# A two-layer hybrid transformer with two gated layers behind it: gate and value products by seven block products, retention and latent values by pairs of heads

## The chip, the cores and the metric

One core of a Trainium2 chip runs the whole program as one kernel. The metric is device time in microseconds of one execution, as a median over runs. Everything is float32; a large product is made of three matmuls of float32r (below), a small one is a plain float32 matmul.

## The reference

512 tokens of width 1024 pass two layers of attention and feed-forward and then two further layers (even and odd), which the change leaves alone. Each attention mixes three heads: a delta-rule recurrence (RWKV-7), a retention of four heads and a latent attention of eight. What the change touches:

```
# retention, four heads of 64, chunks of 128 tokens
inner = einsum('bhnqd,bhnkd->bhnqk', qc, kc) * dmask
inner = einsum('bhnqk,bhnkd->bhnqd', inner, vc)
cross = einsum('bhnqd,nbhde->bhnqe', qc * q_dec, R_prev)    # R_prev: state of the chunks before
# latent attention, eight heads, values of 64, blocks of 128 queries, causal
pr = softmax(s); o = einsum('bhqk,bkhd->bqhd', pr, v)
# feed-forward, D_FF = 2816
gu = rms_norm(h, ffn_norm[l]) @ w_gate_up[l]
h = h + (silu(gu[..., :D_FF]) * gu[..., D_FF:]) @ w_down[l]
```

## The kernel before

Activations stand with channels on the 128 partitions and the 512 tokens as columns. A product `w.T @ x` in full precision is three matmuls (`mm3`): `w` and `x` are each split in a rounded part (`h`) and a rest (`l`), and hh, hl and lh are added in PSUM. Weights come in units of 128 x 1024 (`wunit`): SP issues a transfer of 512 KB into `wr` (two buffers), ScalarE writes the rounded part `wh`, VectorE the rest `wl = wr - wh` (three buffers each). `dense_fm` is one such unit against eight pairs `xh`, `xl`: 24 matmuls of 512 columns into one PSUM bank.

**Feed-forward (`ffn`).** `prenorm` splits the eight channel blocks of `h` and makes the norm's factor, which is spread over the partitions as `RB` (and half of it as `RH`). The 22 blocks of 128 hidden channels go in groups of 8, 8 and 6. For each, one unit gives the gate `pg`, one the value `pu`; VectorE multiplies both, as they leave PSUM, by `RB` and `RH`, ScalarE makes the tanh of the silu, and the result is split (`fah`, `fal`). Behind each group come eight output products of 24 (or 18) matmuls each, added to `h`.

**Retention (`ret_states`, `ret_head`).** Two heads share a tile of 128 partitions. `ret_states` sums the states of the chunks into `R`, 64 columns a chunk. `ret_head` runs for one head: four score matmuls on its 64 partitions (`rsc`), a mask on VectorE, then per chunk one matmul with the state and one with the values into its half of the bank `ro`, and two evacuations by ScalarE.

**Latent attention (`mla_scores`, `mla_values`, `mla_queries`).** Per head and block of 128 queries: scores (`msc`), maximum on VectorE, exponential on ScalarE, normalization on VectorE. When a head has its four blocks, `mla_values` transposes the probabilities by key block (`mpt`) and multiplies them by the 128 value channels of the head's pair (`mo`); of the 128 output rows the head's own 64 are used:

```
self.mm(out[:, c0], st["v"][kb - 1][:, i * P:i * P + P], p0[:, c0], kb == 1, kb == NB)
```

**Order.** The program is written in order, and a scheduler puts instructions on each engine by priority; `high_priority` moves weight preparation (`WPRI`) and evacuations (`EPRI`) ahead. Each engine then runs its own list in order and waits on semaphores. In attention, `weave` puts the steps of the recurrence (`side`) between those of retention and latent attention (`main`). `VAT`, `QAT`, `VDELAY`, `QAHEAD`, `RPOST` say at which steps values, queries and the recurrence's end are issued.

Of the kernel before, what the change touches and what calls it, by code (L numbers as in the profile page):

```python
# [43 lines left out]
WEAVE, VAT, QAT, VDELAY, QAHEAD, RPOST = 1.9, (2, 6, 10, 14), 6, 1, 3, 20  # L44
MSCB, MOB, DB0, DB1, DB2 = ("pa", "pr", "pa", "pr"), "pd", ["pd", "pt"], ["pd"], ["pd"]
# [173 lines left out]
class _Kernel:  # L219
# [145 lines left out]
    def mm(self, out, lhsT, rhs, start, stop):  # L365
        self.nc.tensor.matmul(out=out, lhsT=lhsT, rhs=rhs, start=start, stop=stop)  # L366
# [451 lines left out]
    def rwkv_inverse(self, l, st, eng):  # L818
# [20 lines left out]
        for e in range(2):  # L839
            for hf in range(2):  # L840
                for b, q in enumerate((nc.sync, nc.scalar)):
                    o, i = 64 * hf + 32 * b + 16 * e, 64 * e + 32 * b + 16 * hf
                    q.dma_start(out=tt[i:i + 16, 16 * e:16 * e + 16, 32 * b:32 * b + 32], in_=s2[o:o + 16].rearrange("c i t -> i c t"))
# [155 lines left out]
    def ret_states(self, l, st):  # L999

        st["R"] = []
        for p in range(2):
            ps, kt = self.pt("rkt"), self.t("rkt", "X")
            for j in range(NB - 1):
                self.nc.tensor.transpose(ps[:, j * P:j * P + P], st["k"][p][:, j * P:j * P + P], self.ident)
            self.act(kt[:, :384], ps[:, :384])
            ps = self.pa("rkv")
            R = self.php.tile([P, 192], F32, tag=f"ret_r{p}", name="ret_r", bufs=1)
            for j in range(NB - 1):
                b = slice(j * P, j * P + P)  # L1010
                self.mm(ps[:, b], kt[:, b], st["v"][j][:, p * P:p * P + P], True, True)
                for e in range(2):
                    sl, c = slice(64 * e, 64 * e + 64), slice(64 * j, 64 * j + 64)
                    new = ps[sl, j * P + 64 * e:j * P + 64 * e + 64]
                    if j == 0:
                        self.nc.vector.tensor_copy(R[sl, c], new)
                    else:
                        self.add(R[sl, c], new, R[sl, 64 * j - 64:64 * j])
            st["R"].append(R)

    def ret_head(self, l, st, h):
        p, e = divmod(h, 2)
        sl = slice(64 * e, 64 * e + 64)
        if e == 0:
            st["y"], st["sq"] = st.get("y", []) + [self.t("ry", "M")], st.get("sq", []) + [self.t("rsq", "M")]
        ps, out, s = self.pa("rsc"), self.pt("ro"), self.t("rs", "X")
        k, q = st["k"][p], st["q"][p]
        blocks = [slice(j * P, j * P + P) for j in range(NB)]
        for b in blocks:
            self.mm(ps[:, b], k[sl, b], q[sl, b], True, True)  # L1030
        yield
        self.mul(s[:].rearrange("p (n t) -> p n t", t=P), ps[:].rearrange("p (n t) -> p n t", t=P),
                 self.co("upper").unsqueeze(1).to_broadcast([P, NB, P]))
        yield
        for j, b in enumerate(blocks):
            if j:
                self.mm(out[sl, b], st["R"][p][sl, 64 * j - 64:64 * j], q[sl, b], True, False)
            self.mm(out[sl, b], st["v"][j][:, h * 64:h * 64 + 64], s[:, b], j == 0, True)
        yield
        self.act(st["y"][p][sl], out[sl])  # L1040
        self.act(st["sq"][p][sl], out[sl], AF.Square)
        yield
# [97 lines left out]
    def mla_scores(self, qk, qb):  # L1140
# [3 lines left out]
        ps = self.bank(MSCB[qb], "msc")  # L1144
# [11 lines left out]
    def mla_values(self, l, st, h, prs, mix):  # L1156

        nc = self.nc
        i, e = divmod(h, 2)
        sl = slice(64 * e, 64 * e + 64)  # L1160
        if e == 0:
            mix.append((self.t("mxh", "M", F32R), self.t("mxl", "M", F32R)))
        pair = mix[-1]
        out, last = None, None
        for kb in range(NB + 1):
            if kb < NB:
                ps = self.pt("mpt")
                for qb in range(kb, NB):
                    nc.tensor.transpose(ps[:, qb * P:qb * P + P], prs[qb][:, kb * P:kb * P + P], self.ident)  # L1169
                pt = self.t("mpt", "R")  # L1170
                c = slice(kb * P, T)
                self.act(pt[:, c], ps[:, c])
            if last is not None:
                c0, p0 = last
                if out is None:
                    out = self.bank(MOB, "mo")
                self.mm(out[:, c0], st["v"][kb - 1][:, i * P:i * P + P], p0[:, c0], kb == 1, kb == NB)
            if kb < NB:
                last = (c, pt)
                yield  # L1180
        mh, ml = pair
        self.act(mh[sl], out[sl])
        self.sub(ml[sl], out[sl], mh[sl].bitcast(F32))

    def attn(self, l):
# [30 lines left out]
        def main():  # L1216
# [10 lines left out]
            heads = (x for h in range(4) for x in self.ret_head(l, rst, h))  # L1227
            qk = None
            for i, _ in enumerate(heads):
                if i in VAT:  # L1230
                    self.mla_v(l, mst, VAT.index(i))
                if i == QAT:
                    qk = self.mla_queries(l, mst, 0)
                if i % 4 == 3:
                    yield
# [5 lines left out]
            keys = {0: qk}  # L1241
            probs, vals, post = {}, [], iter(())
            for s in range(32 + VDELAY):
                h, qb = divmod(s, NB)
                if h < 8:
                    if qb == 0:
                        probs[h] = []
                    probs[h].append(self.mla_scores(keys[h], qb))
                if s >= NB + VDELAY and (s - VDELAY) % NB == 0:
                    i = (s - VDELAY) // NB - 1  # L1250
                    vals.append(self.mla_values(l, mst, i, probs[i], mix))
                vals = [v for v in vals if next(v, "end") != "end"]
                if (s + QAHEAD) % NB == 0 and NB <= s + QAHEAD < 32:
                    keys[(s + QAHEAD) // NB] = self.mla_queries(l, mst, (s + QAHEAD) // NB)
# [4 lines left out]
            vals.append(self.mla_values(l, mst, 7, probs[7], mix))  # L1259
# [15 lines left out]

    def ffn(self, l):
        self.dbanks = ["pd", "pt", "pr"]
        xs, rT, RB, RH = self.prenorm(f"ffn_norm{l}", half=True)
        for k0 in range(0, NF, 8):
            n = min(8, NF - k0)  # L1280
            acts = []
            for m in range(k0, k0 + n):
                pg = self.dense_fm(self.a["wgu"][l, 2 * m], xs)
                z = self.t("fz", "Z")
                self.evac(z, pg, RB)
                th = self.t("fth", "Z")
# [511 lines left out]
    def run(self):  # L1798
        self.setup()
        for l in range(L2):  # L1800
            with self.phase("attn", R=26, M=15, I=2):
                self.attn(l)
            with self.phase("ffn", F=40, Z=8):
                self.ffn(l)
# [47 lines left out]
```

## Time and profile before

| | us |
|---|---|
| median of 3 runs (2008.69 to 2012.46) | 2009.08 |
| profiled execution, its own time | 2010.3 |
| span of that execution, first to last instruction | 2008.5 |
| TensorE (PE) busy in the span | 1972.3 |
| VectorE (DVE) busy | 1274.5 |
| ScalarE (ACT) busy | 808.1 |
| GpSimd (POOL) busy | 68.9 |

A row of the timeline has its start, its duration and what it is: line, operation, `out<-in` by the program's names, shape. TensorE's durations overlap, since its matmuls are pipelined: what one costs is read from the starts. Row "x2" merges instructions of one kind. A line can be that of a helper: L285 is any tensor operation of two tensors, L303 one with a scalar besides, L306 any activation, L366 any matmul.

### The profile page before, as it was taken

The numbers are of one execution on the slowest core, as the hardware profiler recorded it, in microseconds if no ns is written. First come the engines' busy times: TensorE is split into PE (matmuls) and PEld (weight loads), VectorE is DVE, ScalarE is ACT, GpSimd is POOL, SyncE is SP. The second block draws the span as 40 slices with busy tenths as digits, with TensorE's granted clock in tenths as the row PEclk, the third lists the DMA queues.
The fourth block names the chain that finished last, engine by engine and source line by source line (L and its number), as shares of the span: only waits on it lengthen the run. The fifth ranks groups of instructions, "written<-read, shape, count | busy, mean of one in ns | idle before, by whom it ended". The sixth has DMA issues, their size and how long they took to land.

```text
span 2008.5 us, 25747 instructions
## 1 busy us (share of the span) xinstructions
PE 1972.3 (98%) x10016; PEld 1582.8 (79%) x10016; DVE 1274.5 (63%) x2367; ACT 808.1 (40%) x1323; POOL 68.9 (3%) x116
## 2 busy tenths in 40 slices
PE   8999999999999999999999999999999999999998
PEld 5777678888888877766788888888888888888886
DVE  7874665544535688647555354458988884389665
ACT  6523553322223444336433222234545453347242
POOL 3100000000000201000000000000000000020000
PEclk9999999999999999999999999999999999999999
DMA  5420122332332523212233233323333323222221
GB/s 178 127 69 23 52 85 91 99 94 95 96 103 87 166 85 102 52 33 70 74 95 95 95 97 103 95 86 98 97 94 98 100 90 112 93 72 84 74 84 43
DMA packets 64910, 180.06 MB, mean 90 GB/s; under 512 B 13892, under 2 KB 16740, under 8 KB 64788
## 3 DMA queue, kind: packets, MB, share of 16 engines
q1 hardware_dynamic: 60528, 175.27, 27.9%
q0 software_dynamic: 1808, 2.69, 0.5%
q8 instruction: 79, 1.29, 0.3%
q10 hardware_dynamic: 2452, 0.45, 0.2%
q14 instruction: 43, 0.35, 0.1%
HBM read 172.29 MB, written 6.09 MB: 89 GB/s over the span
## 4 chain that ended last, share of the span: by engine, by line
PE 81%; DVE 9%; issue 4%; ACT 3%; DMA 2%; POOL 1%; SPq 0%; DVEq 0%; ACTq 0%; POOLq 0%
PE pd L366 68%; PE msc L366 2%; PE mo L366 2%; DVE wl L285 2%; PE egate L366 1%; PE ro L366 1%; PE mpt L1169 1%; DVE xinv L285 1%; DVE xprod L285 1%; ACT wh L306 1%; PE bch L366 1%; DVE xl L303 1%; DMA wr<-owout 1%; PE ost L366 0%; DVE h L285 0%
## 5 line engine op out<-in xcount | busy, mean ns | idle before, releaser
L366 PE MATMUL pd<-xh,wh 128*128 128x512 f32 (+1 forms) x1512 | 591.2, 391 | 8.3 <-ACT xh L306 6.1
L306 ACT ACTIVATE wh<-wr 128x1024 fp32r<-128x1024 f32 (+3 forms) x285 | 296.3, 1040 | 746.7 <-PE pd L366 517.2
L366 PE MATMUL pd<-xl,wh 128*128 128x512 f32 (+1 forms) x1512 | 592.4, 392 | 4.3 <-DVE xl L303 4.1
L366 PE MATMUL pd<-xh,wl 128*128 128x512 f32 (+1 forms) x1512 | 590.2, 390 | 0.0
L285 DVE TENSOR_TENSOR wl<-wr,wh 128x1024 fp32r<-128x1024 f32 (+3 forms) x285 | 341.6, 1199 | 98.1 <-ACT wh L306 97.6
L366 PEld LDWEIGHTS pd<-xh,wh 128*128 128x128 f32 (+1 forms) x1512 | 284.2, 188 | 68.2 <-ACT xh L306 6.5
L366 PEld LDWEIGHTS pd<-xl,wh 128*128 128x128 f32 (+1 forms) x1512 | 284.3, 188 | 66.7 <-DVE xl L303 8.4
L366 PEld LDWEIGHTS pd<-xh,wl 128*128 128x128 f32 (+1 forms) x1512 | 284.4, 188 | 57.3 <-issue 1.0
L285 DVE TENSOR_TENSOR h<-pd,h 128x512 f32<-128x512 f32 x64 | 44.2, 691 | 150.1 <-PE pd L366 150.1
L366 PE MATMUL pd<-fal,wh 128*128 128x512 f32 x352 | 137.2, 390 | 0.0
L366 PE MATMUL pd<-fah,wl 128*128 128x512 f32 x352 | 137.0, 389 | 0.0
L366 PE MATMUL pd<-fah,wh 128*128 128x512 f32 x352 | 136.7, 389 | 0.0
L285 DVE TENSOR_TENSOR fth<-pd,RH 128x512 f32<-128x512 f32 x44 | 30.4, 692 | 118.6 <-PE pd L366 118.6
L366 PE MATMUL pd<-mxh,wh 128*128 128x512 f32 (+1 forms) x272 | 102.8, 378 | 0.0
L366 PE MATMUL pd<-mxh,wl 128*128 128x512 f32 (+1 forms) x272 | 102.6, 377 | 0.0
L366 PE MATMUL pd<-mxl,wh 128*128 128x512 f32 (+1 forms) x272 | 102.5, 377 | 0.0
L285 DVE TENSOR_TENSOR fz<-pd,RB 128x512 f32<-128x512 f32 x44 | 30.4, 692 | 99.3 <-PE pd L366 99.3
L366 PEld LDWEIGHTS pd<-fal,wh 128*128 128x128 f32 x352 | 66.1, 188 | 14.4 <-DVE fal L285 0.7
L366 PEld LDWEIGHTS pd<-fah,wh 128*128 128x128 f32 x352 | 66.0, 188 | 14.0 <-ACT fah L306 0.3
L366 PEld LDWEIGHTS pd<-fah,wl 128*128 128x128 f32 x352 | 66.1, 188 | 13.7
L366 PEld LDWEIGHTS pd<-mxh,wl 128*128 128x128 f32 x272 | 51.2, 188 | 9.3
L366 PEld LDWEIGHTS pd<-mxl,wh 128*128 128x128 f32 x272 | 51.2, 188 | 9.3
(509 smaller groups left out, 2851.4 us busy)
## 6 DMA issues: line engine op xcount, KB each, us to landing
wr<-wgu SPq DMA_DIRECT2D x88, 512.0 KB, 3.5
wr<-ewin SPq DMA_DIRECT2D x48, 512.0 KB, 3.5
wr<-win SPq DMA_DIRECT2D x35, 512.0 KB, 3.6
wr<-wd SPq DMA_DIRECT2D x32, 512.0 KB, 3.5
wr<-wout SPq DMA_DIRECT2D x16, 512.0 KB, 3.5
wr<-ewout SPq DMA_DIRECT2D x16, 512.0 KB, 3.8
wr<-wd SPq DMA_DIRECT2D x16, 384.0 KB, 3.2
h<-xT SPq DMA_DIRECT2D x16, 256.0 KB, 4.9
```

The source lines that it names most:

```text
L285: (eng or self.nc.vector).tensor_tensor(out, x, y, op)
L303: (eng or self.nc.vector).scalar_tensor_tensor(out=out, in0=x, scalar=s, in1=y, op0=op0, op1=op1)
L306: self.nc.scalar.activation(out, x, f, **kw)
L366: self.nc.tensor.matmul(out=out, lhsT=lhsT, rhs=rhs, start=start, stop=stop)
L1169: nc.tensor.transpose(ps[:, qb * P:qb * P + P], prs[qb][:, kb * P:kb * P + P], self.ident)
```

## The change

**Feed-forward.** The tokens are cut in two halves of 256 columns, the input channels in two halves of 512; gate and value weights of a block then are a 2 x 2 matrix of blocks (`a11`, `a12` of the gate, `a21`, `a22` of the value), the input another (`b11` ... `b22`). Strassen's scheme in Winograd's form makes the four results from seven products of sums. `halves` makes the four sums of the input once a layer; `gate_up` makes four sums of the weights per block on GpSimd, splits 3.5 units instead of two, runs seven products of 12 matmuls with 256 columns, and adds the seven results on VectorE. The first two blocks of a layer (`PLAIN`) stay as they were. `fg` has two buffers, `fs` one.

**Retention.** `ret_pair` runs two heads together: the states stand as 128 x 128 blocks with zeros off the diagonal, so that one matmul serves both heads; scores and values of the two heads alternate; the evacuations take both heads at once.

**Latent attention.** A step is one block of queries of a pair of heads. `mla_values` handles one block for both heads: transposes in groups of two key blocks, then one matmul per head and key block with its own 64 value channels, into its half of the bank. `mxh` and `mxl` are made once a pair. Besides, four of the eight transfers of `tt` in `rwkv_inverse` move from ScalarE's queue to GpSimd's.

```diff
-            R = self.php.tile([P, 192], F32, tag=f"ret_r{p}", name="ret_r", bufs=1)
+            R = self.php.tile([P, 384], F32, tag=f"ret_r{p}", name="ret_r", bufs=1)
+            self.nc.gpsimd.memset(R, 0.0)
...
+    def ret_pair(self, l, st, p):
...
+        for b in blocks:
+            for e in range(2):
+                self.mm(pss[e][:, b], k[sl[e], b], q[sl[e], b], True, True)
...
+        for j in range(1, NB):
+            self.mm(out[:, blocks[j]], st["R"][p][:, j * P - P:j * P], q[:, blocks[j]], j == 1, False, skip_group_check=True)
+        for j, b in enumerate(blocks):
+            for e in range(2):
+                h = 2 * p + e
+                self.mm(out[sl[e], b], st["v"][j][:, h * 64:h * 64 + 64], ss[e][:, b], False, True, skip_group_check=True)
...
+    def mla_values(self, st, i, qb, prs, out, mix):
+        for k0 in range(0, qb + 1, 2):
...
+                for e in range(2):
+                    h, o = 2 * i + e, (2 * j + e) * P
+                    self.mm(out[64 * e:64 * e + 64, qb * P:qb * P + P], st["v"][kb][:, h * 64:h * 64 + 64], pt[:, o:o + P],
+                            kb == 0, kb == qb)
...
+    def gate_up(self, l, m, xs, ts, RB, RH):
+        nc, H, pool = self.nc, T // 2, self.nc.gpsimd
+        g = self.php.tile([P, UNIT], F32, tag="fg", name="fg", bufs=2)
+        u = self.wp.tile([P, UNIT], F32, tag="wr", name="wr", bufs=2)
+        S = self.php.tile([P, 3 * T], F32, tag="fs", name="fs", bufs=1)
...
+            self.add(s1, a21, a22, pool)
+            self.sub(a21, a11, a21, pool)
+            self.sub(s2, s1, a11, pool)
+            self.sub(s4, a12, s2, pool)
+            wg, wu, w1 = unit(g), unit(u), self.split(s1, "f1", "W")
+            ws = unit(S[:, T:])
...
+        product(A[:, lo], wg, 0, b11)
+        product(B[:, hi], wg, T, b21)
+        product(A[:, hi], wu, 0, t3)
+        product(C[:, hi], wu, T, t4)
+        product(E[:, lo], w1, 0, t1)
+        product(B[:, lo], ws, 0, t2)
+        product(C[:, lo], ws, T, b22)
...
+            self.act(y[:, 3], A[:, lo])
+            self.add(y[:, 0:3:2], B[:].rearrange("p (s t) -> p s t", t=H), two(y[:, 3]))
+            self.add(y[:, 1], y[:, 0], A[:, hi])
+            self.add(y[:, 0:6:5], y[:, 0:2], two(E[:, lo]))
+            self.add(y[:, 3:5], y[:, 0:2], C[:].rearrange("p (s t) -> p s t", t=H))
...
+        self.mul(z, z, RB)
+        self.act(th, z, AF.Tanh, scale=0.5)
+        self.stt(z, th, 1.0, z, ALU.add, ALU.mult)
+        self.mul(up, up, RH)
+        self.mul(z, z, up)
+        return self.split(z, "fa", "F")
```

Three places of the order, as each engine runs it. On VectorE in a group of the feed-forward, one block before (`fz` and `fth` are gate and value, `fal` the rest of the result):

```order
L285 TENSOR_TENSOR fal<-fz,fah 128x512
L285 TENSOR_TENSOR fz<-pd,RB 128x512
L285 TENSOR_TENSOR wl<-wr,wh 128x1024
L303 SCALAR_TENSOR_TENSOR fz<-fth,fz 128x512
L285 TENSOR_TENSOR fth<-pd,RH 128x512
L285 TENSOR_TENSOR fz<-fz,fth 128x512
L285 TENSOR_TENSOR wl<-wr,wh 128x1024
```

And of the change, from the first PSUM read of a block (`fB`, `fA`, `fE`, `fC` are the banks of the products, `fy` their sums, `f1` the split of the first weight sum):

```order
L288 TENSOR_TENSOR fy<-fB,fy 128x2x256
L288 TENSOR_TENSOR fy<-fy,fA 128x256
L288 TENSOR_TENSOR fy<-fy,fE 128x2x256
L288 TENSOR_TENSOR fy<-fy,fC 128x512
L288 TENSOR_TENSOR wl<-fs,wh 128x1024
L288 TENSOR_TENSOR fy<-fy,RB 128x512
L288 TENSOR_TENSOR fy<-fy,RH 128x512
L288 TENSOR_TENSOR wl<-fg,wh 128x1024
L288 TENSOR_TENSOR f1l<-fs,f1h 128x512
L306 SCALAR_TENSOR_TENSOR fy<-fy 128x512
L288 TENSOR_TENSOR fy<-fy 128x512
L288 TENSOR_TENSOR wl<-wr,wh 128x1024
```

Seven rows a block have become thirteen (`fal` stands behind these twelve): the split of `fs` for the next block follows the last PSUM read, those of `fg` and `wr` for the block after stand between the multiplications.

On GpSimd, which had nothing in the feed-forward before, one block of the change and the start of the next, with the engines waited for:

```order
L288 TENSOR_TENSOR fs<-wr 128x512 [waits DMAHW0_49,DVE_49]
L288 TENSOR_TENSOR wr<-fg,wr 128x512 [waits DMAHW7_49,Pool_49]
L288 TENSOR_TENSOR fs<-fs,fg 128x512
L288 TENSOR_TENSOR fs<-fg,fs 128x512 [waits Pool_49]
L288 TENSOR_TENSOR fs<-wr 128x512 [waits DMAHW2_49,DVE_49]
```

The first sum into `fs` waits for VectorE, the later ones for the transfers and for GpSimd itself.

On TensorE in the first layer's latent attention, the end of a head's values before (`mo`; `mpt` are transposes):

```order
L366 MATMUL pd<-qlh,wsh 128x512
L366 MATMUL mo<-mpt,mv 128x384
L1169 MATMUL mpt<-cst,mp 128x128
L366 MATMUL pd<-qll,wsh 128x512
L366 MATMUL pd<-qlh,wsl 128x512
L366 MATMUL mo<-mpt,mv 128x256
L1169 MATMUL mpt<-cst,mp 128x128
L366 MATMUL mo<-mpt,mv 128x128
```

And of the change, values of a pair:

```order
L369 MATMUL mo<-mpt,mv 64x128 x4
L1174 MATMUL mpt<-cst,mp 128x128 x2
L369 MATMUL msc<-mk,mq 128x256
L369 LDWEIGHTS idb
L369 MATMUL msc<-mskb,idb 128x128
L369 MATMUL msc<-mk,mq 128x384
L369 MATMUL mo<-mpt,mv 64x128 x6
L1174 MATMUL mpt<-cst,mp 128x128 x5
```

The matmuls of 128, 256, 384 and 512 columns with 128 value channels have become runs of matmuls with 64 value channels and 128 columns, two heads in turn, and transposes and scores stand between the runs.

## Rows read from the trace of the kernel before

**Rows 1.** The page: engines' busy us and share; the chain that ended last

```profile
PE 1972.3 (98%) x10016; PEld 1582.8 (79%) x10016; DVE 1274.5 (63%) x2367; ACT 808.1 (40%) x1323; POOL 68.9 (3%) x116
...
PE 81%; DVE 9%; issue 4%; ACT 3%; DMA 2%; POOL 1%; SPq 0%; DVEq 0%; ACTq 0%; POOLq 0%
```

**Rows 2.** Windows, first feed-forward layer: us, busy us (x instructions) by engine

```profile
437.00:524.00 87.00, 87.00 (x386) 72.06 (x385) 40.30 (x48) 23.28 (x27) 0.00 (x0) 1.00 0.30 97
```

**Rows 3.** Timeline of PE, 512 and 256 columns: start, duration, what

```profile
467.69 0.39 PE L366 MATMUL pd<-xh,wh 128*128 128x512 f32 x1
467.92 0.39 PE L366 MATMUL pd<-xl,wh 128*128 128x512 f32 x1
...
1741.04 0.28 PE L366 MATMUL pd<-mxl,wh 128*128 128x256 f32 x1
1741.16 0.28 PE L366 MATMUL pd<-mxh,wl 128*128 128x256 f32 x1
```

**Rows 4.** Groups by form, VectorE, weight splits: busy us, mean ns

```profile
L285 DVE TENSOR_TENSOR wl<-wr,wh 128x1024 fp32r<-128x1024 f32 x260 | 317.7, 1222 | 93.4 <-ACT wh L306 93.0
```

**Rows 5.** Timeline of VectorE, first feed-forward layer, a block's end

```profile
352.29 0.69 DVE L285 TENSOR_TENSOR fth<-pd,RH 128x512 f32<-128x512 f32 x1 [2.69 <-PE pd L366]
353.02 0.69 DVE L285 TENSOR_TENSOR fz<-fz,fth 128x512 f32<-128x512 f32 x1
353.63 1.22 DVE L285 TENSOR_TENSOR wl<-wr,wh 128x1024 fp32r<-128x1024 f32 x1
354.77 0.68 DVE L285 TENSOR_TENSOR fal<-fz,fah 128x512 fp32r<-128x512 f32 x1
```

**Rows 6.** Groups by form, ScalarE, as in rows 4

```profile
L306 ACT ACTIVATE wh<-wr 128x1024 fp32r<-128x1024 f32 x260 | 275.2, 1058 | 690.8 <-PE pd L366 477.2 <-issue 182.4 <-DMA wr<-ewout 8.4
...
L306 ACT ACTIVATE fah<-fz 128x512 fp32r<-128x512 f32 x44 | 27.9, 634 | 28.7 <-DVE fz L285 28.7
```

**Rows 7.** Timelines of VectorE and GpSimd (POOL), start of the kernel

```profile
8.66 0.75 DVE L303 SCALAR_TENSOR_TENSOR xl<-h,vec,xh 128x512 fp32r<-128x512 f32 x1
...
12.16 1.79 DVE L303 SCALAR_TENSOR_TENSOR xl<-h,vec,xh 128x512 fp32r<-128x512 f32 x1
...
9.22 1.33 POOL L285 TENSOR_TENSOR acc<-acc,sq 128x512 f32<-128x512 f32 x1 [6.18 <-ACT sq L306]
...
11.98 1.41 POOL L285 TENSOR_TENSOR acc<-acc,sq 128x512 f32<-128x512 f32 x1 [1.44 <-ACT sq L306]
```

**Rows 8.** Timelines of the same two, before the odd layer's products

```profile
1761.36 0.47 DVE L303 SCALAR_TENSOR_TENSOR xl<-h,vec,xh 128x256 fp32r<-128x256 f32 x1
1761.75 0.47 DVE L303 SCALAR_TENSOR_TENSOR ey<-ey,vec,spread 128x256 f32<-128x256 f32 x1
1762.14 0.68 DVE L303 SCALAR_TENSOR_TENSOR xl<-h,vec,xh 128x256 fp32r<-128x256 f32 x1
...
1761.81 0.73 POOL L285 TENSOR_TENSOR RH<-RH,sq 128x256 f32<-128x256 f32 x1 [0.39 <-ACT sq L306]
```

**Rows 9.** The chain of waits, 170 to 290 us: shares by line

```profile
by line: PE pd L366 27.7%; PE msc L366 14.8%; PE mo L366 14.1%; PE ro L366 7.6%; PE mpt L1169 6.5%; PE bch L366 2.7%; PE rsc L366 2.5%; issue 2.0%; PE g L366 1.8%; PE mch L366 1.7%; ACT mp L306 1.7%; PE rkv L366 1.6%; PE ych L366 1.5%; PE s
```

**Rows 10.** Timeline of PE, attention of the first layer (x2: two passes)

```profile
221.08 1.02 PE L366 MATMUL mo<-mpt,mv 128*128 128x512 f32 x2
221.94 1.02 PE L366 MATMUL msc<-mk,mq 128*128 128x512 f32 x2
...
223.08 0.39 PE L366 MATMUL msc<-mk,mq 128*128 128x128 f32 x2
223.30 0.22 PE L366 MATMUL msc<-mskb,idb 128*128 128x128 bf16 x1
```

**Rows 11.** Timeline of PE, the same layer's recurrent chunks (x4: two matmuls)

```profile
185.97 0.29 PE L366 MATMUL ych<-g,uv 128*64 128x64 f32 x4
186.09 0.29 PE L366 MATMUL ych<-ar,mbd 128*64 128x64 f32 x4
186.31 0.49 PE L366 MATMUL rsc<-rx 64*128 64x128 f32 x2
```

More of the change, by code (lines that the diff above doesn't have):

```diff
@@ L363, in evac, with mm @@
             self.mul(out, ps, y)
-    def mm(self, out, lhsT, rhs, start, stop):
-        self.nc.tensor.matmul(out=out, lhsT=lhsT, rhs=rhs, start=start, stop=stop)
+    def mm(self, out, lhsT, rhs, start, stop, **kw):
+        self.nc.tensor.matmul(out=out, lhsT=lhsT, rhs=rhs, start=start, stop=stop, **kw)
     def mm3(self, out, a, b, first, last):
@@ L840, in rwkv_inverse @@
             for hf in range(2):
-                for b, q in enumerate((nc.sync, nc.scalar)):
+                for b, q in enumerate((nc.sync, nc.gpsimd)):
                     o, i = 64 * hf + 32 * b + 16 * e, 64 * e + 32 * b + 16 * hf
@@ L1019, in ret_states @@
             st["R"].append(R)
[L1021 to L1026, printed above, removed]
+    def ret_pair(self, l, st, p):
+        pss, out = [self.pa("rsc") for _ in range(2)], self.pt("ro")
         k, q = st["k"][p], st["q"][p]
+        sl = [slice(0, 64), slice(64, 128)]
@@ L1154, in mla_scores @@
         return pr
[L1156 to L1183, printed above, removed]
+    def mla_values(self, st, i, qb, prs, out, mix):
+        for k0 in range(0, qb + 1, 2):
+            n = min(2, qb + 1 - k0)
+            ps, pt = self.pt("mpt"), self.t("mpt", "R")
+            for j in range(n):
+                for e, pr in enumerate(prs):
+                    o = (2 * j + e) * P
+                    self.nc.tensor.transpose(ps[:, o:o + P], pr[:, (k0 + j) * P:(k0 + j) * P + P], self.ident)
+            self.act(pt[:, :2 * n * P], ps[:, :2 * n * P])
+            yield
+            for j in range(n):
+                kb = k0 + j
+                for e in range(2):
+                    h, o = 2 * i + e, (2 * j + e) * P
+                    self.mm(out[64 * e:64 * e + 64, qb * P:qb * P + P], st["v"][kb][:, h * 64:h * 64 + 64], pt[:, o:o + P],
+                            kb == 0, kb == qb)
+        if qb == NB - 1:
+            mix.append(self.split(out, "mx", "M"))
     def attn(self, l):
@@ L1240, in main @@
                 pass
[L1241 to L1245, printed above, removed]
-                    if qb == 0:
[L1247 to L1254, printed above, removed]
+            probs, vals, post, out = [], [], iter(()), None
+            for s in range(32 + 2 * VDELAY):
+                step, e = divmod(s, 2)
+                i, qb = divmod(step, NB)
+                if s < 32:
+                    probs.append(self.mla_scores(keys[2 * i + e], qb, e))
+                for d, ahead in enumerate(QAHEAD):
+                    if (s + ahead) % 8 == 0 and 8 <= s + ahead < 32:
+                        h = (s + ahead) // 4 + d
+                        keys[h] = self.mla_queries(l, mst, h)
+                vals = [v for v in vals if next(v, "end") != "end"]
+                if e == 1 and 0 <= step - VDELAY // 2 < 16:
+                    i, qb = divmod(step - VDELAY // 2, NB)
+                    if qb == 0:
+                        out = self.bank(MOB, "mo")
+                    vals.append(self.mla_values(mst, i, qb, probs[2 * (step - VDELAY // 2):][:2], out, mix))
                 if s == RPOST:
@@ L1278, in ffn @@
         xs, rT, RB, RH = self.prenorm(f"ffn_norm{l}", half=True)
+        ts = self.halves(f"ffn_norm{l}")
         for k0 in range(0, NF, 8):
@@ L1802, in run @@
                 self.attn(l)
-            with self.phase("ffn", F=40, Z=8):
+            with self.phase("ffn", F=19, W=4):
                 self.ffn(l)
```

98 lines of the change are left out of this document (73 added, 25 removed).

## The prediction

> **What bounds the kernel now.** I read the page first: TensorE is busy for 98% of the span, and 81% of the chain that ended last is its work [rows 1]. Then the windows by stage: in a stretch of the first feed-forward layer (437 to 524 us) TensorE is busy without a break while VectorE works 40.3 and ScalarE 23.3 of 87 us [rows 2]. So in that stage only less work on TensorE makes the kernel shorter, and the two other engines have room, but not for everything. The timeline gives the price of that work: a matmul of 512 columns starts 0.227 us after the one before it, one of 256 columns 0.12 us [rows 3]. Gate and value of one block of 128 hidden channels are 2 x 24 = 48 matmuls of 512 columns, 48 x 0.2267 = 10.88 us. The attention stage is TensorE's as well: in its second half the chain puts 14.1% of 120 us on the products with the values (`mo`, 16.9 us), 7.6% on the retention outputs (`ro`, 9.1 us) and 2.5% on the retention scores (`rsc`, 3.0 us) [rows 9].
>
> **Feed-forward, TensorE.** In 20 of a layer's 22 blocks seven products of 4 x 3 matmuls of 256 columns take the place of 48 of 512: 84 x 0.12 = 10.08 us against 10.88, a gain of 0.80 us a block, 32 us for 40 blocks. That is all that the seven products can give.
>
> **Feed-forward, what has to keep up.** Per block VectorE has 13 instructions: three splits of 1024 columns, whose durations are 1.22 us [rows 4], and ten smaller ones. By the starts in the timeline a split occupies VectorE for 1.14 us, an operation of 512 columns for 0.61, and for 0.73 where the next one needs its result [rows 5]; the addition of 256 columns is taken at 0.50, from the 0.47 of an operation of that size [rows 8] and the same delay. In the order shown above: 0.73 + 0.50 + 0.73 + 0.61 for the four that read PSUM (2.57), 3 x 1.14 = 3.42 for the splits, 0.73 + 5 x 0.61 = 3.78 for the rest: 9.77 us, where before it had 2 x 1.22 + 5 x 0.69 = 5.9. ScalarE has 3 x 1.06 + 2 x 0.63 + 0.62 + 0.38 = 5.4 us, the 0.62 and 0.38 estimated from the same two rows [rows 6]. Alone, VectorE would just stay under TensorE's 10.08.
>
> It is not alone. Four sums of 512 columns per block go to GpSimd, and there the trace of before has a warning. At 8.66 us VectorE's `xl` takes 0.75 us; at 12.16, beside a GpSimd sum of the same size, 1.79 [rows 7]. At the change to the last layer, `xl` of 256 columns takes 0.47 at 1761.36 but 0.68 at 1762.14, ending 0.28 after the GpSimd sum that began at 1761.81; in between `ey`, one of whose operands is in PSUM (`spread`), runs its normal 0.47 inside that sum [rows 8]. So an operation of VectorE with both tensors in SBUF and a GpSimd sum run one after the other, and one with a PSUM operand is free. In the new block nine of VectorE's 13 have both in SBUF, the three splits among them. A GpSimd sum of 512 columns costs VectorE between 1.04 us (1.79 - 0.75) and 1.33 (the sum's own shortest duration) [rows 7]; I take 1.17, near the middle, since neither row is a clean one: the first may have overlapped by the tail, the second began while `xl` still ran. Four of them: 4.7 us.
>
> The Trainium skill, page "SBUF — State Buffer", section "Who interferes with whom", says that the pair of ports which the two engines share is held for the whole instruction and the other one fully blocks. By that rule each sum would cost its whole 1.33 us; a block would take 15.1 us and the sum below come to 2086. By the rows it is 1.17 and the sum below; the order of the two does not depend on it.
>
> Can the 4.7 us hide in the 2.57 us that read PSUM? The order says no. `fs` has one buffer, so the first sum of the next block waits until VectorE has split `fs`, and this split stands behind `fC`, the last PSUM operation; ahead of the next `fB` stand the split of `wr`, which needs GpSimd's second sum, and six more operations that take turns with the other two. So a block in the steady state takes 9.77 + 4 x 1.17 = 14.45 us, VectorE and GpSimd in turn, and TensorE waits.
>
> Not every block. During the eight output products after each group (8 x 24 x 0.2267 = 43.5 us for a full group) VectorE has 1.14 + 0.61 of every 5.44 us to do, and the order puts the whole preparation of the next block, and of the one after it all but the split of `fs`, into that time. From there a third block just arrives in time (14.45 us against two blocks of 10.08). So three blocks in each of the three groups go at TensorE's pace, 18 in two layers, and 22 at 14.45: 18 x (10.08 - 10.88) + 22 x (14.45 - 10.88) = -14.4 + 78.5 = **+64 us**. With 1.04 per sum it is +53, with 1.33 +78.
>
> **Ends and starts of the groups.** Behind the last product stand `fC`, a split, the multiplication by `RB`, the tanh, two multiplications and the split of the result: 0.73 + 1.14 + 0.69 + 0.62 + 0.69 + 0.69 + 0.63 + 0.68 = 5.9 us. Seven of eight parts of the first output product cover it, 21 x 0.2267 = 4.8 us, in four groups, and 15 x 0.2267 = 3.4 in the two of six blocks: 4 x 1.1 + 2 x 2.5 = **+9 us** (0 to 17). Before, the chain was 3.2 us by the timeline [rows 5] and hidden. At the start of each layer `halves` adds 8 differences and 8 splits on VectorE (8 x 0.34 + 8 x 0.61 = 7.6 us) and 8 differences of 0.73 on GpSimd (5.8 us) [rows 8], beside the two plain blocks of 21.8 us on TensorE, in which VectorE has some 11 us of its own work and the preparation of two blocks: about 5 us too much a layer, **+10** (0 to 20).
>
> **Attention.** A matmul of float32 operands makes two passes; one of 128 columns takes 0.22 us, one of 512 columns 0.86 [rows 10]. Before, each head multiplies by both heads' values and uses half. Now each head has its own 64 channels, and two heads write the two halves. The trace shows that such halves run side by side: four records of 64 columns, which are two matmuls, in 0.12 us [rows 11], where two after one another would take twice that. So the 80 matmuls of a layer are 40 x 0.22 = 8.8 us instead of 16.9, or 17.6 if they do not pair. Against it: the array is split for them and not for the transposes, and a change of form costs: after `ych` the next matmul of another form starts 0.22 us after the last group instead of 0.12 [rows 11], 0.10 more. The order has 20 runs of `mo` in a layer, so 40 changes, 4 us. Values: 16.9 - 8.8 - 4 = 4 us saved. The retention outputs fall from 9.1 to (6 + 8) x 0.22 = 3.1 us, the scores from 3.0 to 8 x 0.22 = 1.8, less about 1 for their changes of form: 6 saved. Ten a layer, **-20 us** in all; the bounds are -37 (no changes of form, all of it on the path) and 0 (the softmax chain takes it back).
>
> The Trainium skill, page "TensorEngine Tiling (Array Packing)", section "Key Properties", says that a change of tiling form drains TensorE. If each drain cost the 0.22 us of a whole small matmul, the 40 changes would be 9 us a layer and the attention -10 us in all; the row shows 0.10 [rows 11].
>
> The four transfers of `tt` per layer that move from ScalarE's queue to GpSimd's I cost at nothing: TensorE works on projections there; without that cover it would be four issues, some 2 us a layer.
>
> **Sum.** +64 + 9 + 10 - 20 = +63 us on the profiled execution's 2010.3, 2073; that execution lies 1.2 us over the median of the runs, so **2072 us**. The lowest and highest ends of the terms give 53 + 0 + 0 - 37 = +16 and 78 + 17 + 20 - 0 = +115.
>
> **Rivals.**
> - *Half of the sums hide.* If GpSimd's third and fourth sums run while VectorE reads PSUM, a block takes 9.77 + 2 x 1.17 = 12.1 us: -14.4 + 22 x 1.2 + 19 - 20 = +12, 2021. For it: these two sums are needed last. Against it: the order, as above. Chance 0.15.
> - *TensorE keeps the pace: faster.* If the sums fall only into time in which VectorE waits, its 9.77 us fit under 10.08, the gain of 32 us is had and the ends stay covered: -32 - 20 = -52, 1957. The place is the steady state of a group; it decides at -14.4 + 22 (x - 10.88) + 19 - 20 = 0, x = 11.6 us a block, so when no more than 1.8 of the 4.7 us show. For it: 46.7 of 87 us of VectorE were idle [rows 2]. Against it: the new work fills them. Chance 0.18.
> - *The halves do not pair.* The values then take 17.6 + 4 us a layer; the attention gives 20 - 2 x 9 = 2 us instead of 20, 2090. Rows 11 speak against it. Chance 0.04.
> - The forecast: 0.63.
>
> **Numbers.** Within 0.2% (4 us, about what a measurement can tell) lies only a sliver of the first rival, 0.03. Faster is the second rival, 0.18; slower the rest, 0.79. The forecast with its bounds spans 2025 to 2125, most of it 2040 to 2112; the first rival reaches down to 2000. From 2000 to 2112 some 8 in 10 are held, the faster case is outside.
>
> **What would show it.** In the changed profile: TensorE with gaps in the groups, ended by VectorE's splits (`wl` of `wr` and `fs`), and none in the first three blocks; blocks 14 to 15 us apart; GpSimd busy for 5 us or more a block; VectorE near full, with splits of 1.22 us lengthened to over 2 beside GpSimd's sums, and `fB` to `fC` at their normal length; matmuls of 256 columns at 0.12 us; `mo` records of two heads a few ns apart. The forecast is wrong if blocks are 10 to 11 us apart with TensorE busy throughout, or if `wl` keeps 1.22 us beside a GpSimd sum.

## The result, and the profile after

| | before | after |
|---|---|---|
| median of 4 runs, us | 2010.47 (2008.69 to 2012.46) | 2104.26 (2099.67 to 2104.50) |
| profiled execution, its own time, us | 2010.3 | 2099.67 |
| its span, us | 2008.5 | 2097.9 |
| mean granted clock of TensorE | 0.998 | 0.976 |

The ratio is 1.0461, 95% interval 1.0442 to 1.0480: slower, as forecast, and inside the range, near its upper end: 94 us more where 63 were forecast (89 between the two profiled executions, which are taken apart below). First the page of the changed kernel: busy us and share by engine, and the chain that ended last, by engine and by line.

```profile
PE 1970.3 (94%) x11624; PEld 1654.2 (79%) x11624; DVE 1598.9 (76%) x2631; ACT 892.1 (43%) x1447; POOL 371.6 (18%) x304
...
PE 56%; DVE 29%; issue 9%; ACT 3%; DMA 2%; POOL 1%; DVEq 0%; SPq 0%; POOLq 0%; ACTq 0%
PE pd L369 43%; DVE fy L288 8%; DVE wl L288 8%; DVE fy L306 3%; DVE f1l L288 2%; PE msc L369 1%; PE egate L369 1%; PE mo L369 1%; PE mpt L1174 1%; DVE fal L288 1%; PE fA L369 1%; PE oo L369 1%; PE fC L369 1%; PE bch L369 1%; ACT oe L309 1%
```

Against [rows 1], TensorE's share of the chain went from 81% to 56%, VectorE's from 9% to 29%: the bound has changed hands, in `fy` and `wl`, which are the feed-forward layers. By the starts of TensorE's matmuls the stages differ so:

| stage (us) | before | after | difference |
|---|---|---|---|
| attention, layer 0, to the norm of the feed-forward layer | 333.1 | 327.4 | -5.7 |
| feed-forward, layer 0 | 356.5 | 407.2 | +50.7 |
| attention, layer 1 | 328.6 | 319.4 | -9.2 |
| feed-forward, layer 1 | 356.3 | 407.7 | +51.4 |
| the rest | 634.0 | 636.2 | +2.2 |

The second group of the first feed-forward layer shows the two paces. Windows (us, then busy us and instructions of PE, PEld, DVE, ACT and POOL, the granted clock, share and GB/s of the transfers), over the second block, the sixth and the seventh, and over 2.4 us behind the group:

```profile
485.50:495.58 10.08, 10.08 (x87) 10.08 (x85) 9.91 (x11) 4.60 (x6) 6.10 (x4) 1.00 0.29 103
535.87:549.96 14.09, 11.97 (x87) 11.67 (x85) 13.88 (x14) 4.99 (x8) 7.14 (x5) 0.88 0.24 76
549.96:563.99 14.03, 11.91 (x86) 11.59 (x85) 13.82 (x14) 4.93 (x8) 7.08 (x5) 0.88 0.26 75
...
586.60:589.00 2.40, 2.40 (x6) 1.92 (x7) 0.58 (x1) 0.38 (x1) 0.00 (x0) 0.50 0.00 0
```

Where TensorE was busy throughout [rows 2], it now is so only in the first blocks of a group; later VectorE is busy for 13.8 of 14.0 us. The seven blocks of this group that have one behind them start 10.07, 10.08, 10.59, 15.57, 14.13, 14.09 and 14.03 us apart. VectorE's timeline over a block:

```profile
559.70 0.69 DVE L288 TENSOR_TENSOR fy<-fy,RB 128x512 f32<-128x512 f32 x1
560.30 1.79 DVE L288 TENSOR_TENSOR fy<-fy,RH 128x512 f32<-128x512 f32 x1
562.01 2.32 DVE L288 TENSOR_TENSOR wl<-fg,wh 128x1024 fp32r<-128x1024 f32 x1
564.25 1.77 DVE L288 TENSOR_TENSOR f1l<-fs,f1h 128x512 fp32r<-128x512 f32 x1
565.95 1.78 DVE L306 SCALAR_TENSOR_TENSOR fy<-fy 128x512 f32<-128x512 f32 x1
567.76 0.69 DVE L288 TENSOR_TENSOR fy<-fy 128x512 f32<-128x512 f32 x1
568.37 1.22 DVE L288 TENSOR_TENSOR wl<-wr,wh 128x1024 fp32r<-128x1024 f32 x1
569.51 0.68 DVE L288 TENSOR_TENSOR fal<-fy,fah 128x512 fp32r<-128x512 f32 x1
570.11 0.69 DVE L288 TENSOR_TENSOR fy<-fB,fy 128x512 f32<-128x512 f32 x1
...
572.08 0.69 DVE L288 TENSOR_TENSOR fy<-fy,fC 128x512 f32<-128x512 f32 x1
572.68 1.22 DVE L288 TENSOR_TENSOR wl<-fs,wh 128x1024 fp32r<-128x1024 f32 x1
```

GpSimd's timeline in the same time:

```profile
559.86 1.67 POOL L288 TENSOR_TENSOR fs<-wr 128x512 f32<-128x512 f32 x1 [6.80 <-DVE wl L288]
561.62 1.63 POOL L288 TENSOR_TENSOR wr<-fg,wr 128x512 f32<-128x512 f32 x1
563.21 2.27 POOL L288 TENSOR_TENSOR fs<-fs,fg 128x512 f32<-128x512 f32 x1
565.56 1.62 POOL L288 TENSOR_TENSOR fs<-fg,fs 128x512 f32<-128x512 f32 x1
```

Four sums, four long VectorE instructions: 1.79 instead of 0.69, 2.32 instead of 1.22, 1.77 and 1.78 instead of 0.68 and 0.69: 1.10 us each. The ends alternate: a sum ends at 561.53, `RH` at 562.09, the next sum at 563.25, the split at 564.33, and so on. From one end to the next it is 1.1 to 1.2 us for each sum and for the split, 0.55 us for each VectorE instruction of 512 columns: one at a time, and the records, which begin earlier, contain the wait for the other engine. The price of a sum is 1.10, and 9.77 + 4 x 1.10 = 14.17 is the 14.1 of the blocks. The other instructions keep the durations of [rows 4, 5]. While GpSimd works, no VectorE instruction that reads PSUM runs; behind its four sums GpSimd stands idle for 6.8 us a block. The Trainium skill, page "SBUF — State Buffer", section "Who interferes with whom", has a VectorE instruction with two SBUF inputs contend with a GpSimd one that reads SBUF; the interleaved ends agree with it.

### The profile page after: what moved, and what is told of

Same layout as the page of the kernel before. It is cut to its first block, busy times and chain, and to the rows that moved or that the text cites. A ratio compares the mean times of both kernels' runs of the same rounds, so it can differ in the third digit from the quotient of the medians.

```text
span 2097.9 us, 29776 instructions
## 1 busy us (share of the span) xinstructions
PE 1970.3 (94%) x11624; PEld 1654.2 (79%) x11624; DVE 1598.9 (76%) x2631; ACT 892.1 (43%) x1447; POOL 371.6 (18%) x304
## 4 chain that ended last, share of the span: by engine, by line
PE 56%; DVE 29%; issue 9%; ACT 3%; DMA 2%; POOL 1%; DVEq 0%; SPq 0%; POOLq 0%; ACTq 0%
PE pd L369 43%; DVE fy L288 8%; DVE wl L288 8%; DVE fy L306 3%; DVE f1l L288 2%; PE msc L369 1%; PE egate L369 1%; PE mo L369 1%; PE mpt L1174 1%; DVE fal L288 1%; PE fA L369 1%; PE oo L369 1%; PE fC L369 1%; PE bch L369 1%; ACT oe L309 1%
## 5 line engine op out<-in xcount | busy, mean ns | idle before, releaser
L369 PE MATMUL pd<-xh,wh 128*128 128x512 f32 (+1 forms) x872 | 344.2, 395 | 8.6 <-ACT xh L309 6.3
L369 PE MATMUL pd<-xl,wh 128*128 128x512 f32 (+1 forms) x872 | 344.6, 395 | 3.7 <-DVE xl L306 3.4
L369 PE MATMUL pd<-xh,wl 128*128 128x512 f32 (+1 forms) x872 | 343.8, 394 | 0.0
L369 PEld LDWEIGHTS pd<-xh,wh 128*128 128x128 f32 (+1 forms) x872 | 165.6, 190 | 43.9 <-ACT xh L309 6.3
L369 PEld LDWEIGHTS pd<-xl,wh 128*128 128x128 f32 (+1 forms) x872 | 165.3, 190 | 41.6 <-DVE xl L306 7.9
L369 PEld LDWEIGHTS pd<-xh,wl 128*128 128x128 f32 (+1 forms) x872 | 165.1, 189 | 33.9 <-issue 2.0
L288 POOL TENSOR_TENSOR fs<-wr 128x512 f32<-128x512 f32 x40 | 64.0, 1601 | 418.3 <-DVE wl L288 220.9
L369 PE MATMUL fA<-th,wl 128*128 128x256 f32 x160 | 54.1, 338 | 47.8 <-DVE wl L288 47.8
L288 DVE TENSOR_TENSOR wl<-fg,wh 128x1024 fp32r<-128x1024 f32 x40 | 86.2, 2155 | 3.2 <-ACT wh L309 3.2
L288 POOL TENSOR_TENSOR fs<-fs,fg 128x512 f32<-128x512 f32 x40 | 85.6, 2139 | 0.0
```

What stands on the lines that cost most here:

```text
L288: (eng or self.nc.vector).tensor_tensor(out, x, y, op)
```

## Experiments

**Is it the sums, and would VectorE do them cheaper?** The sums moved to VectorE, then left out.

```
-        nc, H, pool = self.nc, T // 2, self.nc.gpsimd
+        nc, H, pool = self.nc, T // 2, self.nc.vector
```

> The change with its four weight sums per block on VectorE instead of GpSimd; nothing else. In the changed kernel a steady block takes 14.1 us and four VectorE instructions in it are each 1.10 us longer than alone. Theory A (VectorE and GpSimd take turns on operands in SBUF, so a GpSimd sum costs VectorE 1.10 us): the stretching is gone, the splits take 1.22 us throughout, each sum costs VectorE 0.61, and a block takes 9.77 + 4 x 0.61 = 12.2 us; 22 blocks x 1.9 = 42 us less than the changed kernel, about 2062, and less than that (down to 2040) where more than four blocks of a group then keep TensorE's pace. Theory B (the stretching comes from something else, such as ScalarE or the transfers, and GpSimd's sums only happen to lie beside it): the stretching stays and the sums come on top, 14.1 + 2.4 = 16.5 us a block, about 2155.

Measured: 1988.99 us, ratio to the kernel before 0.9889 (0.9873 to 0.9906): not only 42 but 115 us below the changed kernel, and faster than before. Groups by form on VectorE, 470 to 540 us (busy us, mean ns, idle time before):

```profile
L288 DVE TENSOR_TENSOR wl<-wr,wh 128x1024 fp32r<-128x1024 f32 x7 | 8.5, 1220 | 1.5 <-ACT wh L309 1.5
L288 DVE TENSOR_TENSOR wl<-fs,wh 128x1024 fp32r<-128x1024 f32 x6 | 7.3, 1223 | 0.6 <-ACT wh L309 0.5
L288 DVE TENSOR_TENSOR wl<-fg,wh 128x1024 fp32r<-128x1024 f32 x6 | 7.3, 1220 | 0.2 <-ACT wh L309 0.2
...
L288 DVE TENSOR_TENSOR fs<-fg,fs 128x512 f32<-128x512 f32 x6 | 4.1, 685 | 0.0
```

Theory A holds: every split at 1.22, a sum at 0.69 on VectorE. It gained more because a block of 12.2 us, as worked out there, falls only 2.1 behind TensorE's 10.08 and not 4, so that the lead of prepared blocks lasts for six blocks and not for three or four: 36 of the 40 blocks start at TensorE's pace, and only the seventh and eighth of the middle group start 11.9 and 13.9 us (in layer 1 11.9 and 13.3) behind the one before. A window over the six blocks of the first group (columns as above):

```profile
352.93:413.28 60.35, 60.35 (x504) 60.35 (x503) 60.25 (x87) 28.83 (x37) 0.00 (x0) 1.00 0.31 105
```

VectorE is just as full here, yet TensorE never waits. With it went the stalls behind the groups (1.1 and 1.5 us are left in the two layers) and most of the loss at the start (2 us a layer are left).

The version without the four sums, which computes another result:

```
...
-            self.add(s1, a21, a22, pool)
-            self.sub(a21, a11, a21, pool)
-            self.sub(s2, s1, a11, pool)
-            self.sub(s4, a12, s2, pool)
-            wg, wu, w1 = unit(g), unit(u), self.split(s1, "f1", "W")
-            ws = unit(S[:, T:])
+            wg, wu, w1 = unit(g), unit(u), self.split(a21, "f1", "W")
+            ws = unit(g)
```

> The change without the four weight sums: the products that would take a sum take raw weights (a21, and a11 with a12), so the feed-forward result is another; all splits, products and PSUM additions stay. Theory A (VectorE bounds a steady block, 9.77 us of its own and 4 x 1.10 for GpSimd's sums): VectorE fits under TensorE's 10.08, every block starts 10.1 to 10.6 us after the one before, 22 blocks x 4 = 88 us less than the changed kernel; with the ends of the groups some 2 us shorter each and the starts of the layers some 4, about 2000 (1990 to 2015). Theory B (what bounds the block is the chain from the last product of a block over the additions back to a free buffer, not VectorE's load): blocks stay near 14 us and the time near 2095.

Measured, in one run: 1978.5 us, every block 10.07 or 10.08 us behind the one before it. VectorE's own 9.7 us a block fit; the chain from product to buffer (theory B) is not the bound. It went some 20 us below theory A's 2000, for the reason above: the stalls behind the groups and most of those at the starts went with the slow blocks.

**Can the sums hide where VectorE reads PSUM?**

```
-        S = self.php.tile([P, 3 * T], F32, tag="fs", name="fs", bufs=1)
+        S = self.php.tile([P, 3 * T], F32, tag="fs", name="fs", bufs=2)
...
-            with self.phase("ffn", F=19, W=4):
+            with self.phase("ffn", F=16, W=4):
```

> The change with two buffers for the weight sums (fs) instead of one, so that GpSimd's sums of the next block need not wait for VectorE's split of this block's; the pool of activation tiles falls from 19 to 16 for it. In the changed kernel GpSimd does nothing for 6.8 us of each 14.1, among them the four VectorE operations on PSUM (2.5 us). Theory A (the single buffer keeps the sums out of that time, as the prediction had it): up to two of the four sums move into it, a block takes 9.77 + 2 x 1.10 = 12.0 us and the kernel 22 x 2.1 = 46 us less, about 2058. Theory B (the sums still meet VectorE's operations on SBUF, because GpSimd runs ahead and then waits for the transfers and for the split of its own operands): 14.1 stays, 2104.

Measured: 2074.14 us, ratio 1.0312 (1.0295 to 1.0329), 30 below the change; steady blocks 13.7 us in layer 1. GpSimd's timeline of a block:

```profile
543.54 1.30 POOL L288 TENSOR_TENSOR fs<-wr 128x512 f32<-128x512 f32 x1 [6.79 <-DVE wl L288]
544.92 1.63 POOL L288 TENSOR_TENSOR wr<-fg,wr 128x512 f32<-128x512 f32 x1
546.52 1.71 POOL L288 TENSOR_TENSOR fs<-fs,fg 128x512 f32<-128x512 f32 x1
548.31 2.15 POOL L288 TENSOR_TENSOR fs<-fg,fs 128x512 f32<-128x512 f32 x1
```

and VectorE's beside it:

```profile
542.25 1.22 DVE L288 TENSOR_TENSOR wl<-fs,wh 128x1024 fp32r<-128x1024 f32 x1
543.38 0.68 DVE L288 TENSOR_TENSOR fy<-fy,fC 128x512 f32<-128x512 f32 x1
544.09 1.29 DVE L288 TENSOR_TENSOR fy<-fy,RB 128x512 f32<-128x512 f32 x1
545.31 1.79 DVE L288 TENSOR_TENSOR fy<-fy,RH 128x512 f32<-128x512 f32 x1
547.02 2.29 DVE L288 TENSOR_TENSOR wl<-fg,wh 128x1024 fp32r<-128x1024 f32 x1
```

`fC`, which reads PSUM, runs its normal 0.68 although a sum begins inside it, and this sum takes 1.30 and not 1.67; the next VectorE instruction, both inputs in SBUF, takes 1.29. So the exemption of PSUM readers shows here too, but only half a sum found room in it. GpSimd still waits 6.79 us, by its releaser for the split of `fs`, as before; this split ends at 543.47 and now stands ahead of `fC`, so that the first sum meets `fC`. It lies between the two theories, nearer to B. The lead is no longer than before, the fourth interval of the middle group is again the first slow one (14.2 us instead of 15.6); the gain comes from the slow blocks, whose starts there are 12.9 to 14.4 us apart instead of 14.0 to 15.6. In the two layers the blocks take 32 us less, while the output products behind the last group take some 2.6 us more a layer.

**The ends of the groups.**

```
-                if m >= PLAIN:
+                if PLAIN <= m < k0 + n - 1:
```

> The change, but the last block of each group is done as before (14 to 17 of 22 blocks with seven products). In the changed kernel the first output product after a group stands still for about 4 us and is then run for 1.6 us at the lower clock, because VectorE is still busy with the block before the last when the last product ends. Theory A: that stall (5.4 us in groups of eight, 2 in groups of six, 26 us in two layers) goes nearly all, and six blocks of 14.1 become 10.88 with VectorE less loaded, another 19: about 2104 - 45 = 2059. Theory B (the stall comes from the order of the instructions around the output products, not from VectorE's backlog): the stall stays, and only 19 us go: 2085.

Measured: 2066.02 us, ratio 1.0272 (1.0257 to 1.0287), 38 below the change. The stall is gone: in the trace 11.03 us lie between the last product and the first output matmul, which is the plain block, and no output matmul starts late. So theory A. It gave 7 us less than expected, most of it in the blocks, which became shorter by 8 us in layer 0 and 6 in layer 1 instead of 9.6 each: the last block of the first two groups had taken 12.7 us and not the 14.1 that were counted.

**The starts of the layers.**

```
-        ts = self.halves(f"ffn_norm{l}")
+        ts = None
...
                 if m >= PLAIN:
+                    ts = ts or self.halves(f"ffn_norm{l}")
```

> The change, with the differences of the input (halves) written behind the two plain blocks of a layer instead of ahead of them, so that the chain of the norm's small VectorE instructions (rs_) stands ahead of them and of the first weight sums' splits in VectorE's order; sums on GpSimd as in the change. In the changed kernel TensorE stands still for 6.5 us at the start of each layer until that chain ends, and runs 8 matmuls of 512 columns at 0.43 us after it. Theory A (the chain is late because it takes turns with the differences, their splits and GpSimd's sums): the gap and the slow matmuls go, 7.9 us a layer, 16 in all: 2104 - 16 = 2088. Theory B (the work only moves: VectorE has no room before the first block of seven products, which then waits for the splits of the differences): the same gap stands ahead of the first such block, 2104.

Measured: 2097.28 us, ratio 1.0431 (1.0413 to 1.0450), 7 below the change. The gap is gone from the trace, but the first group's six blocks of layer 0 now take 77.2 us instead of 72.5, the first two of them 29.7 together, the products of the one mixed with those of the other, instead of 20.2: half of A, half of B. The same edit with the sums on VectorE, and then with block 15 plain besides (its line is shown at the end of this section):

> Sums on VectorE and the differences behind the two plain blocks. With the sums on VectorE alone the gap at the start of each layer was 2.2 us. Theory A (the gap comes from the order): it goes, 1989 - 4 = 1985. Theory B (VectorE's load before the first block of seven products bounds): no gain, 1989 or more.

> As the run before it, and besides the last block of the middle group of each layer (the one group with eight blocks of seven products) as before. In the run with the sums on VectorE the last two blocks of that group took 11.9 and 13.9 us. Theory A (VectorE's 12.2 us a block against TensorE's 10.08 has by then used up the lead of the prepared blocks): one such block less and a plain one of 10.88 at the end, 1.8 + 3.0 us less a layer, 1985 - 10 = 1975. Theory B: the last block was slow for a reason of its own (the end of the group), and a plain one there waits as long: 1985.

Both missed: 2012.54 us, ratio 1.0009 (1.0000 to 1.0019), and 2006.31, ratio 0.9977 (0.9968 to 0.9986), so 24 us slower with the differences moved behind, where 4 were to be gained. The gap of 2.2 us went, and the first group of each layer grew from 60.5 to 74 and 75 us (in layer 0 the first two blocks take 28.1 us together, and the next start 10.1, 15.4 and 10.7 us apart). Ahead of the plain blocks the differences cost 2 us; behind them they use up the lead that the first group lives on. The second edit, the plain block, took off 6 us where its theory A had 10.

**The two parts of the change.** The attention part alone, with the four transfers of `tt` moved and not moved, and the feed-forward part alone. First `ffn` as in the kernel before, with its pool:

```
-            with self.phase("ffn", F=19, W=4):
+            with self.phase("ffn", F=40, Z=8):
```

> The attention part of the change alone; the feed-forward layers as before. By the two traces the start of the feed-forward layers comes 5.7 us earlier in layer 0 and 9.2 us earlier from layer to layer in layer 1. Theory (the attention gain is real and independent of the feed-forward change, but smaller than the 20 us predicted): about 15 us under the kernel before, ratio 0.992, with products with the values 12.0 us a layer instead of 18.4 and retention outputs 4 instead of 9.7. Rival (the time saved in TensorE's work is lost again where no feed-forward change follows): within 4 us of the kernel before, ratio 1.000. Prediction's own term: 20 us, ratio 0.990.

Measured: 1999.90 us, ratio 0.9947 (0.9932 to 0.9962): 11 us. Products with the values 12.0 and retention outputs 4.1 us a layer, as stated. From layer 0's last output product to the first of layer 1 it is 8.1 us shorter; in layer 0 only 0.9 are left. The scheduler wrote the layer's opening in another order: TensorE's weight load waits 3.02 us for `rep`, until 65.9 us, which the kernel before hasn't, and retention starts 5.4 us later. The changed kernel has the wait too (until 62.1 us), yet its retention starts only 0.4 us later, so the wait alone is not the reason; that the order is, is likely but not shown.

```
-                for b, q in enumerate((nc.sync, nc.gpsimd)):
+                for b, q in enumerate((nc.sync, nc.scalar)):
```

> The attention part alone with the four transfers of tt per layer left on ScalarE's queue. The prediction costed this move at nothing: then the time is that of the attention part alone, 2000 (within 4 us). If the four issues on ScalarE's queue stand in the way of its work there, 2003 to 2004; if the move to GpSimd's queue cost something, 1996 or less.

Measured: 2004.50 us, ratio 0.9968 (0.9956 to 0.9980). By the medians the move is worth some 4 us rather than nothing, but the intervals of the two ratios overlap, and this run too has another order in layer 0, where 3.2 us of the difference lie (1.1 in layer 1); whether queue or order did it stays open.

The kernel before with `halves`, `gate_up`, `ffn` and this pool of the change:

```
-            with self.phase("ffn", F=40, Z=8):
+            with self.phase("ffn", F=19, W=4):
```

> The feed-forward part of the change alone, the attention as before. If the two parts add up: the change is 93 us over the kernel before, its attention part alone 11 under it, so this is 104 over, 2115, ratio 1.052. If the attention part as it stands in the change gives the 20 us that were predicted: 2011 + 113 = 2124. By the stages of the two traces: 102 us over (61 in the blocks, 26 at the ends of the groups, 16 at the starts of the layers), 2113.

Measured: 2121.76 us, ratio 1.0556 (1.0539 to 1.0574): 111 us over the kernel before. Beside it the attention part takes off 17.5 (2121.8 to 2104.3), alone 11: the two don't quite add up, and the orders of layer 0 differ again.

**A version that beats both.** Sums on VectorE, and block 15 plain.

```
-                if m >= PLAIN:
+                if m >= PLAIN and m != 15:
```

> The change with the sums on VectorE (differences of the input where the change has them) and block 15 of each layer, the last of the middle group, as before. With the sums on VectorE alone that group's last two blocks took 11.9 and 13.9 us, and in the run 'combined' the plain block there ended the group without a stall. Theory A: 4.8 us less a layer, 1989 - 10 = 1979. Theory B (the plain block brings back as much as it saves): 1989.

Measured: 1981.55 us, ratio to the kernel before 0.9853 (0.9838 to 0.9868), granted clock 0.996. 7.4 of the 9.6 us were had.

## Why the prediction was right, and where it was short

**TensorE, seven products: right.** 84 matmuls at 0.12 us, blocks 10.07 and 10.08 us apart where nothing holds them.

**What has to keep up: right.** VectorE's own 9.77 us and the taking of turns hold, with 1.10 a sum, inside the 1.04 to 1.33. The rule of the Trainium skill, page "SBUF — State Buffer", section "Who interferes with whom", counted as the sum's own 1.33, was a fifth too dear: that record is longer than the sum's turn of 1.1 to 1.2 us. The blocks cost 7.2 + 14.2 + 9.3 = 30.7 us a layer, 61 in all, where 64 were forecast. The first three intervals of a group at TensorE's pace (10.07 to 10.6) and the rest at about 14.1 are as in the working, but for the fourth (15.5) and the last block of the first two groups (12.7), which offset each other in part.

**Ends of the groups: the step that failed.** "4 x 1.1 + 2 x 2.5 = +9 us (0 to 17)": measured 5.4, 5.4 and 1.5 in layer 0 and 5.5, 5.5 and 1.9 in layer 1, 25 in all, beyond the bound. The chain was counted from the last product on, with `fC` at once, as if VectorE then were free and `fB`, `fA` and `fE` done. VectorE's timeline behind the last product of the middle group, which starts at 576.57:

```profile
576.88 0.69 DVE L288 TENSOR_TENSOR fy<-fy 128x512 f32<-128x512 f32 x1
577.49 1.22 DVE L288 TENSOR_TENSOR wl<-wr,wh 128x1024 fp32r<-128x1024 f32 x1
578.62 0.69 DVE L288 TENSOR_TENSOR fal<-fy,fah 128x512 fp32r<-128x512 f32 x1
579.22 0.68 DVE L288 TENSOR_TENSOR fy<-fB,fy 128x512 f32<-128x512 f32 x1
...
581.19 0.69 DVE L288 TENSOR_TENSOR fy<-fy,fC 128x512 f32<-128x512 f32 x1
581.79 1.22 DVE L288 TENSOR_TENSOR wl<-wr,wh 128x1024 fp32r<-128x1024 f32 x1
...
586.48 0.69 DVE L288 TENSOR_TENSOR fal<-fy,fah 128x512 fp32r<-128x512 f32 x1 [0.69 <-ACT fah L309]
```

and TensorE's:

```profile
582.39 0.39 PE L369 MATMUL pd<-fal,wh 128*128 128x512 f32 x1
586.50 0.80 PE L369 MATMUL pd<-fah,wh 128*128 128x512 f32 x1 [3.73 <-ACT fah L309]
587.10 0.63 PE L369 MATMUL pd<-fah,wl 128*128 128x512 f32 x1
587.53 0.63 PE L369 MATMUL pd<-fah,wh 128*128 128x512 f32 x1
...
589.58 0.39 PE L369 MATMUL pd<-fah,wh 128*128 128x512 f32 x1
```

An engine that bounds the steady state is behind when it ends: VectorE still had the block before to finish and an output weight to split, and came to `fB` 2.5 us and to `fC` 4.5 us behind the last product. From `fC` to the end of `fal` it took 6.0 us, as worked out (5.9); the 4.5 ahead of it are what the sum left out, and TensorE stands still for 3.9 us. Then its matmuls of 512 columns start 0.43 us apart for 3 us, granted clock 0.50 in the window above, 1.5 us more. The prediction had no term for that. That the backlog makes the stall is shown: it went with a plain last block, and with the sums on VectorE.

**Starts of the layers: right in size, wrong in place.** +16 measured, +10 forecast (0 to 20). It was put down to too much work for VectorE beside the two plain blocks; it is one wait inside them, after 45 of their 96 matmuls, for the norm's factor, whose twelve small instructions take turns with the differences, the splits and the sums:

```profile
331.86 1.25 DVE L303 TENSOR_SCALAR rs_ipre<-rs_wpre 128x4 f32<-128x4 f32 x1
333.15 0.17 DVE L288 TENSOR_TENSOR rs_ipre<-rs_ipre,rs_wpre 128x4 f32<-128x4 f32 x1
333.26 2.30 DVE L288 TENSOR_TENSOR wl<-wr,wh 128x1024 fp32r<-128x1024 f32 x1
335.48 1.23 DVE L306 SCALAR_TENSOR_TENSOR rs_ypre<-rs_ipre,rs_ypre 128x4 f32<-128x4 f32 x1
```

Such an instruction of four columns takes 0.16 us alone. The first of these rows reads one tensor only, and it too ends with the GpSimd sum beside it (at 333.11; the sum starts at 331.28 and takes 1.81): the waits are not limited to instructions with two tensors in SBUF, of which alone the prediction spoke. The chain to `rT` took 2.3 us before and takes 13.2; TensorE waits 6.3 for it, and its next six matmuls start 0.37 to 0.57 apart, 1.3 more.

**Attention: right in mechanism.** -20 forecast, -15 by the stages, -17.5 by the runs beside the feed-forward part and -11 alone. All `mo` records of the changed kernel:

```profile
L369 PE MATMUL mo<-mpt,mv x320: 272/273/324, 219.9 to 1007.5; 128*64 128x128 f32 x160
```

80 matmuls of two passes a layer, in pairs. The two records of a pair start 7 ns apart. They occupy TensorE for 12.0 us instead of 18.4, 0.30 a pair: one matmul's 0.22 [rows 10] and most of the 0.10 for a change of form [rows 11]. The other side of the changes is in the transposes and scores, +2.5. That is 3.9 saved a layer where 4 were forecast, and 5.7 in the retention's outputs and scores where 6 were. The 3.9 owe something to luck: the values had occupied 18.4 us and not the 16.9 of [rows 9], and if the +2.5 is the price of the changes of form too, which no run shows by itself, they cost 5.7 us and not 4. The bound of -37 does not come out of the rows: (16.9 - 8.8) + (9.1 - 3.1) + (3.0 - 1.8) is 15.3 a layer, -31. Layer 1 gave 9.2 of 10; in layer 0 part was lost, probably in the opening.

**`tt` at nothing:** perhaps 4 us gained, open as said. **Sum:** +61 + 25 + 16 - 15 + 2 = +89 against +63, the 2 being the rest of the kernel; of the 26, 16 are the ends, 6 the starts and 5 the attention.

**The rivals.** "TensorE keeps the pace" did not happen here; with the sums on VectorE, another kernel, it nearly did. Its point, 11.6 us a block, was too strict, because it holds the lead at three blocks, and a lead lasts longer when a block is less late: 12.2 us a block gave a faster kernel. "Half of the sums hide" needs more than a second buffer. That the halves don't pair is excluded by the 0.30 a pair.

## What to carry to other kernels

An elementwise operation given to GpSimd is not free for VectorE: here a sum cost VectorE 1.10 us where doing it itself costs 0.61, so look at what VectorE runs beside it before moving anything (the Trainium skill, page "Perfetto Trace Analysis", section "Optimizing Scalar/DVE Operations", warns that moving work between these two might not help; the runs agree). An engine that is over its share in part of a loop is paid for by the work prepared ahead: small deficits vanish, larger ones come back with a stall at the end, counted from its backlog and not from a free engine. Where seven products save 7% of TensorE's work, spend them only on as many blocks as the other engines can feed.

## What was not expected of the hardware

A stall cost more than its length: behind waits of 3.7 and 6.1 us TensorE ran for about 3 us at the lower of its two levels, 1.2 GHz (0.43 us for 512 columns where 0.227 is normal), and also inside the steady blocks, behind a wait of 2.1 us, where 256 columns start 0.21 us apart and the clock granted over a block is 0.88. There it seems to cost nothing, since the chain of waits over that block has no work of TensorE in it; where TensorE is the bound, it added 1.3 to 1.5 us to each long wait.
